# A two-block transformer on one core: load buffers on 512-byte boundaries, routing reordered, last output columns in smaller pieces

## The chip, the cores and the metric

The kernel runs as one launch on one core of a Trainium2 chip. The core has a matrix engine (PE, with its weight loads shown apart as PEld), a vector engine (DVE), a scalar engine (ACT), GpSimd (POOL) and SyncE (SP), which here only starts DMAs; 16 DMA engines carry them. Tiles live in SBUF, 128 partitions wide; matmuls write PSUM. Each engine runs its own instructions in order and waits on semaphores. The metric is the device time of one execution in microseconds (us), lower is better.

## The reference

The input is x, 256 tokens by 1024 features, float32. Two transformer blocks follow each other, and what the second one ends with matters here:

```python
x = first_block(x, ...)            # FFN, latent and stick-breaking attention, FFN, gated projection
merged = sigmoid(gate_a) * (y_attn @ w_attn_branch) + sigmoid(gate_b) * (y_ssd @ w_ssd_branch)
x = x + merged @ w_out
x = x + hier_moe(rmsnorm(x, ffn_norm), w_route_group, b_route_group, w_route_expert,
                 b_route_expert, w_gate, w_up, w_down)

def hier_moe(h, ...):              # 4 groups of 8 experts
    g_idx = argmax(h @ w_rg + b_rg)                # one group for each token
    top_v, top_i = top_k(e_logits[g_idx], 2)       # two experts of that group
    combine = group probability * softmax(top_v)
    for e in experts:                              # w_gate, w_up [1024, 256], w_down [256, 1024]
        out += (silu(h @ w_gate[e]) * (h @ w_up[e]) * combine[:, e]) @ w_down[e]
```

Each expert's three matrices are 1 MB each in float32, so the 32 experts are 96 MB, and all of it is read once.

## The kernel before

Tokens are two tiles of 128 (t = 0 and 1). Up to about 972 us the kernel computes both blocks up to `w_out_2`; its matmuls split each float32 operand in a high and a low part and run three products (`mm3`, L219 to L221). The norms of all stages use `rstd` (L137): one DVE step, a power on POOL (L142), and three small DVE steps (L144 to L147).

Then come the experts, in eight quads (q = 0 to 7) of four. SP issues their 192 loads of 512 KB (`moe_loads`, L1381; those of the last quad's `w_down` at L1378) into 32 rotating buffers: 14 from the heap, 8 halves of `raw` tiles and 10 `w4` tiles. Eight loads are in flight at a time, and when all 32 buffers hold weights the next load waits until PE has used a buffer. The order is gate and up of quad 0, then gate and up of quad q and down of quad q-1, and down of quad 7 last.

Before quad 0 can begin, the tokens must be routed. `gemm_out` (L301) computes the last projection `w_out_2`; its last four slices of the contraction (`late=4`) are done for t = 0 first and then for t = 1, so that the routing of t = 0 runs while PE still computes t = 1. `Route.feed` (L1395) takes each finished tile h (L384): a sum of squares on ACT, transposes on PE and copies to `xT` (L1406), `rstd`, the logits matmul (L1411), the logits `lg` (L1418), and the split of h in `hfh` (ACT, L1413) and `hfl` (DVE, L1421). `choose` (L1475) picks group and experts in small DVE steps: the first maximum of the group logits (`first_of`, L852), a penalty on the other groups, the two largest (`tops`, `rest`, `sel`), a running count by matmul (L1496, L1498), `mark`, a permutation matrix `perm` (L1429), and softmax weights (`ex`, `den`, `cw`, L1506 to L1516). `gather` (L1432) multiplies the split h with `perm` (L1447), 16 matmuls of 128x256 for each t, and gives each expert's tokens as `xg`. `gate_up` (L1546) begins at L1558. Where no `keep` pins it, a scheduler chooses the order of each engine's instructions when the program is built.

At the end, `down` (L1584) of quad 7 computes the 1024 output columns in two halves of 512 (L1595 to L1604). For each half it loads four pieces of 512 KB, multiplies (L1602), and `spread` (L1571) splits the result in `yh` (ACT, L1574) and `yl` (DVE, L1575), multiplies both back to token order (L1578, L1579), adds to h (L1580) and starts two output DMAs from ACT's queue (L1582).

```python
            return w.rearrange("(h p r) f -> h p (r f)", p=128, r=4)
...
            self.choose(t, lg, lambda: keep(V.tensor_tensor(hl, h, hh.bitcast(F32), op=ALU.subtract)))
            by_c = lambda z: [z[:, 512 * h:512 * h + 512].rearrange("p (q r) -> p r q", r=4)[:, r, :] for h in range(2) for r in range(4)]
```

The first line lays a gate or up matrix out for its loads; the others show that a 128x128 slice of `hfh` or `hfl` is read by `gather` with every fourth column.

## Time and profile before

| | |
|---|---|
| median of 3 runs | 1241.85 us (1241.27 to 1242.71) |
| the profiled run, its own time | 1240.49 us |
| span of the profiled execution | 1238.4 us |
| mean granted clock of PE | 0.987 |
| PE busy | 1166.7 us, 94% of the span |
| DVE, ACT, POOL busy | 765.9, 579.1, 70.9 us |
| q1, the queues of the large loads | 259.45 MB, 59.1% of 16 engines' span |

PE is busy in nearly all of the span, but the share is a mean over two parts. Up to some 972 us there are matmuls without a break; after it the loads of the experts fill the DMA engines, and PE works on what has landed. The span lacks about 2 us of the profiled run's time, which lie before and after it.

### The profile page before, as it was taken

To read this page: it belongs to the slowest core of one execution; us is meant where nothing else is said; L and a number is where in the kernel's file an instruction comes from. 1 tells how busy PE (TensorE), PEld (TensorE's weight loads), DVE (VectorE), ACT (ScalarE), POOL (GpSimd) and SP (SyncE) were. 2 spreads that over 40 slices of the span, in tenths; PEclk is the share of its full clock that TensorE was granted. 3 is DMA by queue.
4 is the path that set the end of the run, shared out by engine and by line. 5 is a ranking of instruction groups with operands and counts; after the bars stand their busy time and mean duration, and the time that the engine had idled before them with its cause. 6 is when DMAs were issued, how large, how long until landed. Compare 5 with 4: busy or idle time off the path is not lost.

```text
span 1238.4 us, 18312 instructions
## 1 busy us (share of the span) xinstructions
PE 1166.7 (94%) x7106; PEld 916.5 (74%) x7107; DVE 765.9 (62%) x1431; ACT 579.1 (47%) x946; POOL 70.9 (6%) x117
## 2 busy tenths in 40 slices
PE   6999999999999999999998899999999999797877
PEld 5888888977778788888776788898778876352422
DVE  6677747776457676764789777899786552121212
ACT  5555535456565555543654476666444321010100
POOL 2000001110000500000000200000100000000000
PEclk9999999999999999999999899999999989999999
DMA  9563754563334755475542434334754799999997
GB/s 339 185 202 116 261 172 146 177 201 121 119 119 154 206 183 187 140 250 188 193 145 102 170 129 140 107 137 146 178 187 149 284 358 397 408 409 408 408 409 268
DMA packets 105451, 266.22 MB, mean 215 GB/s; under 512 B 8597, under 2 KB 15937, under 8 KB 105361
## 3 DMA queue, kind: packets, MB, share of 16 engines
q1 hardware_dynamic: 102912, 259.45, 59.1%
q0 software_dynamic: 1728, 4.00, 1.4%
q10 hardware_dynamic: 720, 1.57, 0.3%
q8 instruction: 57, 0.93, 0.3%
q14 instruction: 34, 0.27, 0.1%
HBM read 263.95 MB, written 1.05 MB: 214 GB/s over the span
## 4 chain that ended last, share of the span: by engine, by line
PE 50%; DMA 14%; DVE 8%; issue 2%; POOL 2%; ACT 1%; DVEq 0%; POOLq 0%; SPq 0%; ACTq 0%
PE mm L219 7%; PE mm L221 7%; PE mm L220 7%; DMA wq<-in_w_up_dram 4%; DMA wq<-in_w_down_dram 3%; DMA wq<-in_w_gate_dram 2%; DVE lo L203 2%; PE mm L293 2%; PE at L293 2%; DMA raw<-in_w_gate_dram 2%; PE mm L1088 2%; DMA raw<-in_w_down_dram 2%; PE mm L1089 2%; PE mm L1090 2%; POOL r L142 1%
## 5 line engine op out<-in xcount | busy, mean ns | idle before, releaser
L203 DVE TENSOR_TENSOR lo<-raw,hi 128x1024 fp32r<-128x1024 f32 (+3 forms) x312 | 366.2, 1180 | 178.3 <-ACT hi L202 174.0
L202 ACT CAST hi<-raw 128x1024 fp32r<-128x1024 f32 (+3 forms) x312 | 316.0, 1016 | 284.3 <-PE o L220 95.3
L293 PE MATMUL mm<-x,hi 128*128 128x512 f32 x272 | 99.8, 400 | 2.9 <-DVE x L175 2.9
L219 PE MATMUL mm<-hi,xah 128*128 128x512 f32 x192 | 78.4, 409 | 2.7 <-DVE zs L1244 2.6
L142 POOL TENSOR_TENSOR r<-ms,phalf 128x1 f32<-128x1 f32 (+2 forms) x40 | 39.4, 984 | 725.7 <-DVE ms L140 720.4
L1558 PE MATMUL at<-wq,xg 128*32 128x256 f32 x736 | 63.5, 391 | 15.3 <-DMA wq<-in_w_up_dram 11.3
L294 PE MATMUL mm<-x,lo 128*128 128x256 f32 x272 | 76.3, 282 | 0.1
L221 PE MATMUL mm<-hi,xal 128*128 128x512 f32 x192 | 75.6, 394 | 0.3 <-DVE xal L175 0.3
L220 PE MATMUL mm<-lo,xah 128*128 128x512 f32 x192 | 75.6, 394 | 0.2 <-DVE ms L140 0.2
L293 PE MATMUL at<-x,hi 128*128 128x512 f32 x192 | 70.2, 392 | 0.0
L293 PEld LDWEIGHTS mm<-x,hi 128*128 128x128 f32 x272 | 51.8, 191 | 15.2 <-DVE x L175 3.5
L1558 PEld LDWEIGHTS at<-wq,xg 128*32 128x32 f32 x736 | 28.4, 112 | 43.9 <-DMA wq<-in_w_up_dram 19.4
L1088 PE MATMUL mm<-xah,hi 128*128 128x256 f32 x192 | 57.6, 300 | 3.2 <-ACT sq L957 3.2
L1568 DVE SCALAR_TENSOR_TENSOR act<-at,cg,sa 128x256 f32<-128x256 f32 x8 | 5.3, 663 | 89.3 <-ACT sa L1565 89.3
L293 PE MATMUL tp<-x,hi 128*128 128x512 f32 x160 | 59.0, 392 | 0.0
L1089 PE MATMUL mm<-xal,hi 128*128 128x256 f32 x192 | 55.9, 291 | 0.0
L1090 PE MATMUL mm<-xah,lo 128*128 128x256 f32 x192 | 55.3, 288 | 0.0
L294 PE MATMUL at<-x,lo 128*128 128x256 f32 x192 | 53.5, 278 | 0.0
L294 PEld LDWEIGHTS mm<-x,lo 128*128 128x128 f32 x272 | 51.9, 192 | 0.8 <-DVE lo L203 0.8
L1565 ACT ACTIVATE sa<-at,rs 128x256 f32<-128x256 f32 x8 | 3.8, 474 | 103.4 <-PE at L1558 74.9
L221 PE MATMUL mm<-hi,gxl 128*128 128x512 f32 x132 | 51.6, 391 | 0.0
L220 PE MATMUL mm<-lo,gxh 128*128 128x512 f32 x132 | 51.6, 391 | 0.0
(575 smaller groups left out, 2735.5 us busy)
## 6 DMA issues: line engine op xcount, KB each, us to landing
raw<-in_w_in_dram SPq DMA_DIRECT2D x50, 1024.0 KB, 4.9
raw<-in_ffn_w_in_dram SPq DMA_DIRECT2D x40, 1024.0 KB, 5.0
wq<-in_w_down_dram SPq DMA_DIRECT2D x52, 512.0 KB, 10.2
wq<-in_w_up_dram SPq DMA_DIRECT2D x48, 512.0 KB, 10.2
raw<-in_ffn_w_out_dram SPq DMA_DIRECT2D x22, 1024.0 KB, 5.1
wq<-in_w_gate_dram SPq DMA_DIRECT2D x44, 512.0 KB, 10.2
raw<-in_w_gate_dram SPq DMA_DIRECT2D x20, 512.0 KB, 10.2
raw<-in_w_out_dram SPq DMA_DIRECT2D x8, 1024.0 KB, 4.9
```

The lines of the kernel that those rows point to most:

```text
L142: G.tensor_tensor(out=r0, in0=ms, in1=phalf[:, :n], op=ALU.pow)
L202: first(S.copy(hi, part))
L203: first(V.tensor_tensor(lo, part, hi.bitcast(F32), op=ALU.subtract))
L219: PE.matmul(ps, xh, wh, start=first, stop=False)
L220: PE.matmul(ps, xh, wl, start=False, stop=False)
L221: PE.matmul(ps, xl, wh, start=False, stop=last)
L293: PE.matmul(ps[f], hi[:, c, s], sx.both[k // 2][:, :, k % 2, :], start=(k == 0), stop=False)
L294: PE.matmul(ps[f][:, 1, :], lo[:, c, s], sx.hi(k), start=False, stop=(k == KC - 1))
L1088: PE.matmul(o, hi[:, c, s], xh, start=(k == 0 and f % 2 == 0), stop=False)
L1089: PE.matmul(o, hi[:, c, s], xl, start=False, stop=False)
L1090: PE.matmul(o, lo[:, c, s], xh, start=False, stop=(k == 7 and f % 2 == 1))
L1558: PE.matmul(pg[s, n * 256:n * 256 + 256], xg[k // 4][:, k % 4, c:c + CAP], ws[j][:, r * 256:r * 256 + 256], start=(n + k == 0), stop=(n + ...
```

## The change

Seven edits, in the order of the program:

- A tile `pad` of 448 bytes in each partition, used by nothing, stands first in the constants. With the other changes of constants it moves the first address of the pools `weights` and `heap` from 96 bytes past a multiple of 512 (25184 and 98912) to a multiple of 512 (25600 and 99328), and with it all load buffers, since their sizes are multiples of 512.
- `rstd` for one column: POOL also computes `q`, minus half of the power, and DVE needs two steps after the power where it needed three.
- `w_out_2` runs with `late=5`.
- Routing: group logits and expert logits begin at columns 0 and 8 of 40; the first maximum is found by the same MAX, MEMSET and MATCH_REPLACE steps as the two best experts; nearly all of these DVE steps are pinned in program order; the softmax weights of both tiles (`weigh`) come after the routing of t = 1; the `hfl` of t = 1 comes in two halves.
- The split h is stored in chunks, so that `gather` reads each 128x128 slice contiguously; ACT's copy and DVE's subtraction now read h with a stride of 8 elements. The order of the contraction changes with it, so the gate and up loads take 4 KB out of every 8 KB, as the down loads did before.
- The last quad's down works on columns 0 to 511, 512 to 767 and 768 to 1023: four loads of 512 KB, then twice four of 256 KB, whose contiguous runs in DRAM are 2 KB and 1 KB. Six output DMAs replace four.
- POOL sets the widened `wr` and `br` and no longer writes `rev`.

```diff
+TAKEN, ABSENT = -3.0e38, 3.0e38
...
+    cp.tile([128, 112], F32, name="pad")
...
+        if n == 1:
+            q, u, r = small([128, 1], name="q"), small([128, 1], name="u"), small([128, 1], name=name)
+            G.tensor_scalar(q, r0, -0.5, None, op0=ALU.mult)
+            pin(V.scalar_tensor_tensor(u, r0, r0, ms, op0=ALU.mult, op1=ALU.mult))
+            pin(V.scalar_tensor_tensor(r, u, -3.0, q, op0=ALU.add, op1=ALU.mult))
+            return r
...
-        run(gemm_out(mx2, a["w_out_2"], 8, consume, fin))
+        run(gemm_out(mx2, a["w_out_2"], 8, consume, fin, late=5))
...
-        wr = heap([128, 8, 36], name="wr")
+        wr = heap([128, 8, 40], name="wr")
+        G.memset(wr, 0.0)
...
-        G.dma_start(g_exp.rearrange("p (h r) -> p h r", h=2), a["ffn_norm_2"].rearrange("(h p r) -> p h r", p=128, r=4))
-        br = cp.tile([128, 36], F32, name="br")
...
+        G.dma_start(g_exp, a["ffn_norm_2"].rearrange("(p c) -> p c", p=128))
...
+    LAST = [slice(0, 512), slice(512, 768), slice(768, 1024)]
...
-    def rows_of(w, what="gu"):
-
-        if what == "gu":
-            return w.rearrange("(h p r) f -> h p (r f)", p=128, r=4)
+    def rows_of(w):
+
         return w.rearrange("(p r) f -> p (r f)", p=128)
...
+            ws = []
...
                         if (q, what) == (7, "d"):
-                            src = a[nm][e // 8][e % 8].rearrange("(p r) f -> p r f", p=128)
-                            keep(nc.sync.dma_start(w.rearrange("p (r f) -> p r f", r=2), src[:, :, half * 512:half * 512 + 512]))
+                            ws.append(w)
+                            continue
                         else:
-                            src = rows_of(a[nm][e // 8][e % 8], what)
-                            keep(nc.sync.dma_start(w, src[half] if what == "gu" else src[:, half * 1024:half * 1024 + 1024]))
+                            src = rows_of(a[nm][e // 8][e % 8])
+                            keep(nc.sync.dma_start(w, src[:, half * 1024:half * 1024 + 1024]))
                         yield w
+        for i, c in enumerate(LAST):
+            n = c.stop - c.start
+            for j in range(4):
+                w = ws[4 * (i > 0) + j][:, 512 * (i > 1):][:, :2 * n].rearrange("p (r f) -> p r f", r=2)
+                e = 28 + j
+                keep(nc.sync.dma_start(w, a[NAMES[2]][e // 8][e % 8].rearrange("(p r) f -> p r f", p=128)[:, :, c]))
+                yield w
...
-            if t == 1:
+
+            chunks = lambda z: z.rearrange("p (c q) -> p c q", c=8)
+            rows = h.rearrange("p (q c) -> p c q", c=8)
+            self.hi[t], self.lo[t] = chunks(hh), chunks(hl)
+
+            def rest(c):
+                keep(V.tensor_tensor(self.lo[t][:, c], rows[:, c], self.hi[t][:, c].bitcast(F32), op=ALU.subtract))
+
+            keep(S.copy(self.hi[t], rows))
+            if t == 0:
+                rest(slice(0, 8))
+            else:
                 self.first = self.gather(0, ("mm", "mm", "mm", "o"))
                 next(self.first)
...
+            self.weigh[t] = self.choose(t, lg, lambda: [rest(slice(c, c + 4)) for c in (0, 4) if t])
+            if t == 1:
+                for weigh in self.weigh:
+                    weigh()
...
-                    pin(PE.matmul(ps[k // 2][:, k % 2, :], src[t][k], P[t],
+                    pin(PE.matmul(ps[k // 2][:, k % 2, :], src[t][:, k, :], P[t],
...
+            flat = lambda z: z.rearrange("p g e -> p (g e)")
+
+            def firsts(x, n, name):
+
+                top, rest = small([128, 8], name="tops"), small([128, x.shape[1]], name=name)
+                keep(V.max(out=top, in_=x))
+                keep(V.memset(top[:, n:], ABSENT))
+                keep(V.match_replace(out=rest, in_to_replace=top, in_values=x, imm_value=TAKEN))
+                return top, rest
+
+            gtop, grest = firsts(lg[:, :8], 1, "grest")
             pen = small([128, 4], name="pen")
-            V.tensor_scalar(pen, first_of(gl, gmax, 4, rev), -1.0, -NEG, op0=ALU.add, op1=ALU.mult)
-            flat = lambda z: z.rearrange("p g e -> p (g e)")
+            keep(V.tensor_scalar(pen, grest[:, :4], 0.5 * TAKEN, NEG, op0=ALU.is_gt, op1=ALU.mult))
...
+            top, rest = firsts(flat(ml), 2, "rest")
...
             mark = self.mark[t] = small([128, 32], name="mark")
-            V.scalar_tensor_tensor(mark, sel, -float(FAR), pr, op0=ALU.mult, op1=ALU.add)
+            keep(V.scalar_tensor_tensor(mark, sel, -float(FAR), pr, op0=ALU.mult, op1=ALU.add))
             self.perm(t, 0)
             then()
...
+            def weigh():
+
...
+            return weigh
...
-            yh, yl = heap([128, 512], FR, name="yh"), heap([128, 512], FR, name="yl")
+            n = c.stop - c.start
+            yh, yl = heap([128, n], FR, name="yh"), heap([128, n], FR, name="yl")
...
+                for piece in LAST:
+                    y = mm()[:, :piece.stop - piece.start]
                     ws = [next(loads) for _ in range(4)]
                     for i in range(5):
                         for j, c in ((i, 0), (i - 1, 1)):
                             if 0 <= j < 4:
-                                PE.matmul(y[slot(j), :], aT[:, c, slot(j)], ws[j][:, cols[c]], start=(c == 0), stop=(c == 1))
-                    spread(y, back, cols[nb], True)
+                                PE.matmul(y[slot(j), :], aT[:, c, slot(j)], ws[j][:, c, :], start=(c == 0), stop=(c == 1))
+                    spread(y, back, piece, True)
                 return
             y = [mm() for _ in range(2)]
             for c in range(2):
```

In DVE's row from the last part of h of t = 1 on (h_5538, tiles 9614 to 9632 belong to t = 1, the others to t = 0), before:

```order
L384 SCALAR_TENSOR_TENSOR h_5538<-o_9387,h_5538 128x512
L1429 TENSOR_TENSOR perm_9570<-mark_9568,marks 128x256
L1421 TENSOR_TENSOR hfl_9539<-h_5537,hfh_9538 128x1024
L1512 TENSOR_TENSOR ex_9580<-ex_9580,sel_9564 128x32
L1406 COPY xT_9616<-tp_9618 128x512
L1513 TENSOR_REDUCE den_9581<-ex_9580 128x1
L1406 COPY xT_9616<-tp_9625 128x512
L1514 TENSOR_TENSOR den_9581<-den_9581,gs_9578 128x1
L1515 RECIPROCAL den_9581<-den_9581 128x1
L1516 TENSOR_SCALAR cw_9543<-ex_9580,den_9581 128x4x8
L1407 TENSOR_TENSOR ss_9614<-ss_9614 128x1
L140 TENSOR_SCALAR ms_9632<-ss_9614 128x1
```

and now (h_5551, tiles 9620 to 9644 belong to t = 1):

```order
L393 SCALAR_TENSOR_TENSOR h_5551<-o_9412,h_5551 128x512
L1501 MEMSET tops_9575 128x6
L1413 COPY xT_9622<-tp_9624 128x512
L1502 MATCH_REPLACE rest_9576<-tops_9575,ml_9573 128x32
L1413 COPY xT_9622<-tp_9631 128x512
L1512 TENSOR_SCALAR sel_9580<-rest_9576 128x32
L1414 TENSOR_TENSOR ss_9620<-ss_9620 128x1
L143 TENSOR_SCALAR ms_9638<-ss_9620 128x1
L1519 SCALAR_TENSOR_TENSOR mark_9584<-sel_9580,at_9582 128x32
L149 SCALAR_TENSOR_TENSOR u_9643<-r_1942_9640,ms_9638 128x1
L1447 TENSOR_TENSOR perm_9586<-mark_9584,marks 128x256
L150 SCALAR_TENSOR_TENSOR r_9644<-u_9643,q_9642 128x1
```

Before, t = 0's `perm`, its `hfl` and its softmax weights stood between h and `ms` of t = 1; now only the end of t = 0's choice does, and `mark` and `perm` of t = 0 stand behind `ms`.

In PE's row from the logits of t = 1 to its gather, before (the lines left out are the other 11 matmuls of t = 0's gather; four more stood ahead of the logits):

```order
L1411 MATMUL at_9641<-wr_3819,xT_9616 128x36 x8
L1447 MATMUL mm_9653<-perm_9570,hfh_9538 128x256
...
L1528 MATMUL tp_9813<-cw_9543,perm_9570 128x9
L1538 MATMUL tp_9826<-ident,perm_9570 128x128
L1496 LDWEIGHTS before
L1496 MATMUL at_9700<-sel_9698,before 128x32
L1498 LDWEIGHTS ones
L1498 MATMUL at_9700<-sel_9564,ones 128x32
L1447 MATMUL mm_9653<-perm_9705,hfh_9650 128x256 x2
```

and now (left out: 15 more matmuls of t = 0's gather):

```order
L1514 LDWEIGHTS before
L1514 MATMUL at_9582<-sel_9580,before 128x32
L1418 MATMUL at_9648<-wr_3828,xT_9622 128x40 x8
L1465 MATMUL mm_9660<-perm_9586,hfh_9558 128x256
...
L1514 LDWEIGHTS before
L1514 MATMUL at_9702<-sel_9700,before 128x32
L1516 LDWEIGHTS ones
L1516 MATMUL at_9702<-sel_9580,ones 128x32
L1465 MATMUL mm_9660<-perm_9707,hfh_9657 128x256 x2
```

The count of t = 0 (`at_9582`) moved from ahead of the end of the projection to just ahead of t = 1's logits, and all 16 matmuls of t = 0's gather now stand between the logits and the count of t = 1. The matmuls for slot weights (L1528, L1538) left this place for one behind quad 0's gate matmuls.

In ACT's row at the end of the program, from the first piece of the last quad on, before:

```order
L1574 CAST yh_11184<-mm_11167 128x512
L1582 DMA out_dram<-h_5537 128x512
L1582 DMA out_dram<-h_5538 128x512
L1574 CAST yh_11215<-mm_11198 128x512
L1582 DMA out_dram<-h_5537 128x512
L1582 DMA out_dram<-h_5538 128x512
```

and now:

```order
L1596 CAST yh_11206<-mm_11185 128x512
L1604 DMA out_dram<-h_5550 128x512
L1604 DMA out_dram<-h_5551 128x512
L1596 CAST yh_11233<-mm_11220 128x256
L1604 DMA out_dram<-h_5550 128x256
L1604 DMA out_dram<-h_5551 128x256
L1596 CAST yh_11260<-mm_11247 128x256
L1604 DMA out_dram<-h_5550 128x256
L1604 DMA out_dram<-h_5551 128x256
```

The copy `yh` of each later piece stands behind the two output DMAs of the piece before it, now twice.

## Rows read from the trace of the kernel before

**Rows 1.** The page, part 2: GB/s moved in each of 40 slices of 30.96 us

```profile
GB/s 339 185 202 116 261 172 146 177 201 121 119 119 154 206 183 187 140 250 188 193 145 102 170 129 140 107 137 146 178 187 149 284 358 397 408 409 408 408 409 268
```

**Rows 2.** Windows: length, busy us (pieces) of PE, PEld, DVE, ACT, POOL; PEclk, DMA share, GB/s

```profile
840.00:842.00 2.00, 2.00 (x19) 2.00 (x18) 2.00 (x6) 1.05 (x1) 1.34 (x2) 1.00 0.47 174
1012.00:1014.00 2.00, 2.00 (x11) 2.00 (x10) 1.04 (x6) 0.00 (x0) 0.00 (x0) 0.50 1.04 414
1014.00:1022.00 8.00, 8.00 (x124) 4.94 (x127) 1.38 (x2) 1.68 (x4) 0.00 (x0) 0.87 0.60 213
1022.00:1030.00 8.00, 8.00 (x135) 4.62 (x131) 1.26 (x5) 2.34 (x3) 0.00 (x0) 1.00 1.00 363
```

**Rows 3.** Waits of SP's queue from 900 us on: total us, times, longest us

```profile
SPq L1381 <- PE at L1558: 13.3, 14, 9.2
```

**Rows 4.** Timeline of DVE, 1000 to 1016.5 us: start, us, engine, line, operation

```profile
1001.53 0.69 DVE L384 SCALAR_TENSOR_TENSOR h<-o,h 128x512 f32<-128x512 f32 x1
1005.72 0.15 DVE L140 TENSOR_SCALAR ms<-ss 128x1 f32<-128x1 f32 x1
1006.60 0.16 DVE L144 SCALAR_TENSOR_TENSOR u<-r 128x1 f32<-128x1 f32 x1 [0.73 <-POOL r L142]
1007.26 0.26 DVE L1418 SCALAR_TENSOR_TENSOR lg<-at,r,br 128x36 f32<-128x36 f32 x1
1009.61 0.18 DVE L1494 TENSOR_SCALAR sel<-rest 128x32 bf16<-128x32 f32 x1
1010.63 0.42 DVE L1429 TENSOR_TENSOR perm<-mark,marks 128x256 fp32r<-128x256 f32 x1
1010.98 1.22 DVE L1421 TENSOR_TENSOR hfl<-h,hfh 128x1024 fp32r<-128x1024 f32 x1
```

**Rows 5.** Timeline of PE, 1000 to 1016.5 us

```profile
1004.55 2.27 PE L1411 MATMUL at<-wr,xT 128*128 128x36 f32 x16
1010.11 0.23 PE L1496 MATMUL at<-sel,before 128*128 128x32 bf16 x1
1011.20 1.76 PE L1447 MATMUL mm<-perm,hfh 128*128 128x256 f32 x6 [0.83 <-DVE perm L1429]
1013.51 1.73 PE L1447 MATMUL mm<-perm,hfl 128*128 128x256 f32 x6
1015.66 1.04 PE L1558 MATMUL at<-wq,xg 128*32 128x256 f32 x12
```

**Rows 6.** Timeline of PE, 840 to 842 us: 128x256 matmuls with contiguous weights

```profile
840.02 0.28 PE L1089 MATMUL mm<-xal,hi 128*128 128x256 f32 x1
840.14 0.28 PE L1090 MATMUL mm<-xah,lo 128*128 128x256 f32 x1
```

**Rows 7.** Timeline of PE, 1219 to 1238.4 us

```profile
1227.25 3.16 PE L1602 MATMUL mm<-wq,aT 128*32 128x512 f32 x16
```

**Rows 8.** Timeline of ACT and its DMA queue, 1219 to 1238.4 us

```profile
1227.85 0.93 ACTq L1582 DMA_DIRECT2D out_dram<-h  x2
1230.50 0.59 ACT L1574 CAST yh<-mm 128x512 fp32r<-128x512 f32 x1 [4.70 <-DMA out_dram<-h]
```

**Rows 9.** Timeline of DVE, 1219 to 1238.4 us

```profile
1233.02 0.68 DVE L1580 TENSOR_TENSOR h<-mm,h 128x512 f32<-128x512 f32 x1
```

**Rows 10.** Windows, in the last loads (columns as in group 2)

```profile
1218.00:1220.00 2.00, 2.00 (x7) 0.52 (x4) 0.44 (x1) 0.78 (x2) 0.00 (x0) 1.00 1.05 387
```

**Rows 11.** The page, part 5: line, operation, count; busy us, mean ns; idle before

```profile
L142 POOL TENSOR_TENSOR r<-ms,phalf 128x1 f32<-128x1 f32 (+2 forms) x40 | 39.4, 984 | 725.7 <-DVE ms L140 720.4
```

**Rows 12.** Groups by line, 1000 to 1016 us: a small POOL operation

```profile
L1420 POOL COPY cw<-r 128x4 f32<-128x4 f32 x1 | 0.2, 192 | 0.6 <-DVE need L1479 0.6
```

**Rows 13.** Waits of PE over the span: total us, times, longest us

```profile
PE tp L166 <- DVE hg L365: 8.3, 2, 7.5
```

**Rows 14.** The page, part 6: DMA issues, KB each, median us to landing

```profile
wq<-in_w_down_dram SPq DMA_DIRECT2D x52, 512.0 KB, 10.2
wq<-in_w_gate_dram SPq DMA_DIRECT2D x44, 512.0 KB, 10.2
```

More of the change, by code (lines that the diff above doesn't have):

```diff
@@ L849, in ple @@
         return hn
-    def first_of(x, m, n, rev):
-        eq = small([128, n], name="eq")
-        V.scalar_tensor_tensor(eq, x, m, rev[:, :n], op0=ALU.is_equal, op1=ALU.mult)
-        top = small([128, 1], name="top")
-        V.tensor_reduce(out=top, in_=eq, axis=AX.X, op=ALU.max)
-        oh = small([128, n], name="oh")
-        V.tensor_scalar(oh, eq, top, None, op0=ALU.is_equal)
-        return oh
     def block2_consts():
@@ L1401, in feed @@
             for i, c in enumerate(halves):
-                S.activation(junk[:, c], h[:, c], AF.Square, accum_out=ss[:, i:i + 1])
+                keep(S.activation(junk[:, c], h[:, c], AF.Square, accum_out=ss[:, i:i + 1]))
                 p = tp()
@@ L1405, in feed @@
                     PE.transpose(p[:, j, :], h[:, i * 512 + j * 128:i * 512 + (j + 1) * 128], ident)
-                V.tensor_copy(xT[:, 4 * i:4 * i + 4, :], p)
-            V.tensor_tensor(ss[:, 0:1], ss[:, 0:1], ss[:, 1:2], op=ALU.add)
-            r = rstd(ss[:, 0:1], 1, D)
-            ps = at((128, 36))
+                keep(V.tensor_copy(xT[:, 4 * i:4 * i + 4, :], p))
+            keep(V.tensor_tensor(ss[:, 0:1], ss[:, 0:1], ss[:, 1:2], op=ALU.add))
+            r = rstd(ss[:, 0:1], 1, D, pin=keep)
+            ps = at((128, 40))
             for k in range(8):
@@ L1475, in choose @@
         def choose(self, t, lg, then):
[L1476 to L1482 removed]
+            before, ones = self.consts[2:4]
+            flat = lambda z: z.rearrange("p g e -> p (g e)")
[6 more added lines that the diff above has]
+            gtop, grest = firsts(lg[:, :8], 1, "grest")
             pen = small([128, 4], name="pen")
[L1484 to L1485 removed]
+            keep(V.tensor_scalar(pen, grest[:, :4], 0.5 * TAKEN, NEG, op0=ALU.is_gt, op1=ALU.mult))
             ml = heap([128, 4, 8], name="ml")
[L1487 to L1492 removed]
+            keep(V.tensor_tensor(ml, lg[:, 8:].rearrange("p (g e) -> p g e", g=4), bc(pen[:, :, None], [128, 4, 8]), op=ALU.add))
+            top, rest = firsts(flat(ml), 2, "rest")
             sel = self.sel[t] = small([128, 32], BF, name="sel")
[L1494 removed]
+            keep(V.tensor_scalar(sel, rest, 0.5 * TAKEN, None, op0=ALU.is_lt))
             pr = at((128, 32))
@@ L1595, in down @@
             if q == 7:
-                for nb in range(2):
-                    y = mm()
+                for piece in LAST:
+                    y = mm()[:, :piece.stop - piece.start]
                     ws = [next(loads) for _ in range(4)]
```

84 lines of the change are left out of this document (33 added, 51 removed).

## The prediction

> **What bounds the kernel now.** I read the GB/s row of the page first. From about 960 us to the end the DMA engines move 408 to 409 GB/s in nearly every slice [rows 1]: here the experts' loads set the time, and a matmul saved counts only if a load starts earlier for it. The one dent is slice 33. The windows show it: 213 GB/s from 1014 to 1022 us, 363 from 1022 to 1030 [rows 2]. Against 409 the first lacks 8 x (1 - 213/409) = 3.8 us of transfer, the second 0.9. The waits of SP name the cause: a load waits 9.2 us for PE at L1558 [rows 3], the first gate matmul. All 32 buffers are full, and quad 0 cannot begin before the tokens are routed. It begins at 1015.66 [rows 5]. So the start of L1558 is the point to follow; each microsecond by which it comes earlier is a microsecond of the run, until the dent is gone (3.8 us).
>
> I count from H, the end of h of t = 1, 1001.53 + 0.69 = 1002.22 [rows 4]. Before: `ms` at H + 3.5, `lg` at H + 5.04, `sel` at H + 7.4 [rows 4], count of t = 1 at H + 7.9, first matmul of t = 1's gather at H + 9.0, L1558 at H + 13.44 [rows 5].
>
> The second place is the end: the last down matmuls start at 1227.25 and take 3.16 us [rows 7], `yh` follows at 1230.50 [rows 8], the last addition ends at 1233.02 + 0.68 = 1233.70 [rows 9], then the output leaves. Up to some 972 us PE works without a break, and small edits on other engines count only where it waits.
>
> **The routing.** First DVE. Between H and `ms` the change takes out `perm` and `hfl` of t = 0 (0.42 and 1.22 us, [rows 4]) and five small steps of its softmax weights, some 0.2 us each (`lg` to `sel` is 2.35 us for 13 steps, [rows 4]); with overlap of their ends that is 2.4 us. It puts in a MEMSET, a MATCH_REPLACE and `sel` of t = 0, 0.7 us. `ms` moves from H + 3.5 to about H + 1.8, the power's answer comes 0.88 later (1005.72 to 1006.60, [rows 4]), and with `perm` of t = 0 (0.42) and one step less DVE could write `lg` at H + 3.5.
>
> Then PE, which is now late instead. The count of t = 0 stands ahead of the logits of t = 1, and it waits for `sel` of t = 0, which DVE writes behind both `xT` copies, about H + 1.7. Behind that wait stand the logits matmuls, 2.27 us [rows 5], and with them `lg`: H + 1.7 + 0.3 + 2.27 = H + 4.3, 0.75 us earlier than before and not 1.5.
>
> Next, all 16 matmuls of t = 0's gather stand between these logits and the count of t = 1. Before, 12 did, and four ran while PE had nothing else. What one costs decides, and there are two prices. Before, each stands about 0.24 us behind the one ahead of it, six in 1.73 us with the tail of the last [rows 5], at a clock of 0.50 in the window of 1012 to 1014 [rows 2]. Other 128x256 matmuls, whose weights are contiguous as these now will be, follow each other by 0.12 us at a clock of 1.00 [rows 2, 6].
> - Dear end, 0.24: gather of t = 0 to H + 8.1, count of t = 1 at H + 8.1 (0.2 later than before), first gather matmul 1.09 us behind it as before (1010.11 to 1011.20, [rows 5]), 16 matmuls of 0.24 = 3.8: L1558 at H + 13.0. Gain 0.4 us, all of it from the transposes L1538 that no longer stand inside this gather.
> - Cheap end, 0.12: gather of t = 0 to H + 6.2; now `sel` sets the count, `lg` + 2.35 = H + 6.65; `perm` ends 0.94 later (1010.11 to 1011.05, [rows 4, 5]), H + 7.6; the two halves of `hfl` (0.61 each, half of 1.22, [rows 4]) to H + 8.85; four more matmuls and the copies: L1558 at about H + 9.6. Gain 3.8 us, the whole dent.
>
> Which price holds hangs on the clock in this stretch. It was 0.50 at 1012 to 1014, and PE had waited often before that (0.83 us just ahead of 1011.20, [rows 5]); in the changed order it still waits between H and the logits. That speaks for the dear end for t = 0's part; for t = 1's part either can hold. I take the middle, **2.1 us**, and keep both ends. `late=5` gives t = 0 five slices of the projection as cover instead of four; its DVE work has all of t = 1's slices beside it, so I cost it at nothing. If its choice were late, the count of t = 0 would hold the logits by as much. The stride in ACT's copy and in `hfl`: nothing shows its price; if `hfl` took twice its 1.22, the dear end would not move, since its second half would be read at H + 11.4, about when PE gets to it.
>
> **The last columns.** The last loads carry runs of 2 KB at 387 GB/s [rows 10] where 4 KB runs moved at 409: 5% dearer. Halving the run once more should add about twice that to the last 2.1 MB: 5.4 us grow by 0.55. In return the last round on 256 columns instead of 512 is shorter: the matmuls behind the last load by about 0.85, `yh`, `yl` and the additions by 0.2, 0.3 and 0.5 (halves of their column-dependent parts). Unhindered that would be 1.3 us better. But the pieces form a chain: PE multiplies piece 2 only behind the spread of piece 1 (before, 1227.25 is just behind the first half's spread), and ACT copies `yh` of a piece only behind the output DMAs of the piece before, which wait for its additions (1227.85 + 0.93 = 1228.78, [rows 8]). Two such links instead of one: piece 2's `yh` at about 1228.8, its DMAs until about 1231.2, piece 3's `yh` then, 0.7 us **later** than today's 1230.50; from there to the last addition 2.1 instead of 3.2 us, so 1233.3 instead of 1233.7. With a shorter last DMA I take **0.6 us** gain, between 1.3 better and 0.5 worse.
>
> **`rstd`.** POOL's `q` runs beside DVE's `u`. Another small POOL step took 0.19 us [rows 12], as long as the DVE step saved; then each site gains about 0.15 us. If `q` took as long as a power (mean 0.98, [rows 11]), a site would lose 0.5. It counts where PE waits for a norm, some five places ([rows 13] holds two of them, 7.5 us at the start, most of it loading). I take **0.3 us** gain, between 0.8 better and 2.5 worse. POOL's `memset`s lie early and are covered.
>
> **The pad** only moves addresses. The nearest rows are the stream itself: 409 GB/s in steady state, 414 in its best 2 us here [rows 1, 2]. The stream of 192 loads, 100.7 MB, takes 246 us, so that difference would be 3.0 us; a loss has no reason. No row shows a transfer with another offset, and I take 0.
>
> The Trainium skill speaks for more: "DMA: Bandwidth & Descriptors", section "How a descriptor splits into AXI transactions", says that transactions start at 256-byte boundaries and that the bytes in front cost beats too. By it a 4 KB run at an offset of 96 would cost 131 beats instead of 128, an estimate of 2.3% or 5.6 us of the stream. The trace neither confirms nor denies it; the same page gives 408.7 GB/s for a lone load stream of 4 KB rows, which is this trace's rate, without saying at which offset.
>
> **The sum.** 1240.49 - 2.1 - 0.6 - 0.3 = 1237.5 against the profiled run's own time. That run lies 1.36 us under the median of 1241.85, so the forecast is 1238.9 us, 0.24% less. About 0.2% (2.5 us) is what a measurement of this kernel can tell from no change, so the forecast lies just beyond that bound.
>
> **Rivals.**
> 1. The wait moves to PE and nothing is gained at the dent: t = 0's gather at the dear price between logits and count. Then L1558 gains 0.4, the end perhaps 0.4: about 1241.0, no change. For it: the clock row and PE's order. Against: 16 contiguous weight loads. Chance 0.27.
> 2. The pad speeds up the stream: 3.0 us more by the rows' best stretch, 1235.9. For it: the stream is the bound for 246 us. Against: a rate so even that nothing in the rows points to waste. Chance 0.12. By the beats of the Trainium skill's page ("DMA: Bandwidth & Descriptors") it would be an estimated 1233.3.
> 3. The new layout slows the stream. 128 of the 192 loads now take 4 KB out of every 8 instead of one contiguous block. The last loads, which also skip, are the slower ones [rows 10]. If that were due to skipping and not to the short runs, 128 x 1.28 us (524,288 bytes at 409 GB/s) = 164 us would grow by up to 5.4%, 8.9 us: about 1247.8. It decides from 3.4% on (5.6 us), where the result turns slower by 2.5 us. Against: down loads skip in the same way already and land in 10.2 us like the gate loads [rows 14]. Chance 0.07.
> 4. The edits do what they say, but the routing is not what SP waits for: excluded by rows 3 and 5, unless another buffer is late; no chance of its own.
>
> **How the numbers follow.** Forecast 0.54, its own range 1237.0 to 1241.0, two thirds of it more than 2.5 us below 1241.85. Faster by over 0.2%: 0.54 x 0.67 + 0.12 + a little of rival 1 = 0.52. Slower: rival 3 and half of `rstd`'s bad end, 0.08. The rest, 0.40, is no change. The range of 8 in 10 takes in the forecast, rival 1 and most of rival 2: 1234.2 to 1242.6.
>
> **What would show it.** Right: L1558 starts at H + 10 to H + 13, the 8-us window behind it loses 1.5 to 3 us of transfer instead of 3.8, the steady rate stays at 408 to 409, and ACT's last `yh` begins at the end of an output DMA. Wrong: a steady rate above 411 (the pad counts) or below 405 (the layout counts), the logits of t = 1 waiting beyond H + 2.3, or `hfl` of t = 1 running past the gather's high part.

## The result and the profile after

The changed kernel takes 1236.05 us (median of 6 runs, 1232.96 to 1238.9), the kernel before in the same session 1241.56. The ratio is 0.9947, 95% interval 0.9932 to 0.9962: 5.5 us in the medians and 0.5% by the ratio faster. The forecast was 1238.9 with a range of 1234.2 to 1242.6. The profiled run took 1233.61 us, its span 1231.9 (before 1238.4). One further run of the kernel with contiguous blocks (below) took 1428.05 us at a mean granted clock of 0.751, and no figure here counts it.

The GB/s row of the page shows the first thing that the forecast did not have:

```profile
GB/s 344 185 202 122 255 173 147 176 200 125 120 113 151 195 201 178 135 253 199 176 169 71 171 138 138 137 103 141 188 184 155 220 416 418 418 417 419 418 419 252
```

Where [rows 1] had 408 to 409 there is now 416 to 419 in every slice of the steady stream (the 33rd to the 39th), and the dent of the 33rd slice is gone. The windows of the kernel after (columns as in [rows 2]) show both, and a new shallow place at the start of the stream:

```profile
974.00:980.00 6.00, 6.00 (x32) 5.03 (x31) 6.00 (x9) 3.01 (x4) 0.00 (x0) 1.00 0.91 289
1004.00:1014.00 10.00, 8.60 (x94) 7.48 (x97) 7.86 (x35) 3.04 (x11) 0.60 (x3) 1.00 1.03 414
1014.00:1022.00 8.00, 8.00 (x136) 6.32 (x132) 0.80 (x5) 2.02 (x3) 0.00 (x0) 1.00 1.03 417
1050.00:1100.00 50.00, 41.57 (x292) 18.29 (x287) 12.18 (x24) 5.46 (x11) 0.00 (x0) 1.00 1.03 418
```

The granted clock (the column before the last two) is 1.00 in the routing, 1004 to 1014. From 974 to 980 the DMA engines move 289 GB/s; before it was 406.

The routing on PE, in the timeline of the kernel after (start, duration, then the wait ahead of it):

```profile
1003.24 0.18 PE L1514 MATMUL at<-sel,before 128*128 128x32 bf16 x1 [0.94 <-DVE sel L1512]
1003.26 1.96 PE L1418 MATMUL at<-wr,xT 128*128 128x40 f32 x16
...
1007.47 0.18 PE L1514 MATMUL at<-sel,before 128*128 128x32 bf16 x1 [0.27 <-DVE sel L1512]
...
1008.50 0.95 PE L1465 MATMUL mm<-perm,hfh 128*128 128x256 f32 x6 [0.83 <-DVE perm L1447]
...
1010.51 0.50 PE L1465 MATMUL mm<-perm,hfl 128*128 128x256 f32 x2 [0.30 <-DVE hfl L1426]
...
1011.18 0.64 PE L1579 MATMUL at<-wq,xg 128*32 128x256 f32 x8
```

and the steps of DVE that it waits for:

```profile
994.85 2.07 DVE L1426 TENSOR_TENSOR hfl<-h,hfh 128x1024 fp32r<-128x1024 f32 x1
...
1000.92 0.67 DVE L393 SCALAR_TENSOR_TENSOR h<-o,h 128x512 f32<-128x512 f32 x1
...
1005.26 0.26 DVE L1435 SCALAR_TENSOR_TENSOR lg<-at,r,br 128x40 f32<-128x40 f32 x1 [0.44 <-PE at L1418]
...
1007.93 0.42 DVE L1447 TENSOR_TENSOR perm<-mark,marks 128x256 fp32r<-128x256 f32 x1
1008.27 2.19 DVE L1426 TENSOR_TENSOR hfl<-h,hfh 128x512 fp32r<-128x512 f32 x2
```

H is 1000.92 + 0.67 = 1001.59, and the first gate matmul (L1579, formerly L1558) starts at 1011.18 = H + 9.59. In [rows 4, 5] it was H + 13.44.

The end, ACT's timeline of the kernel after:

```profile
1217.57 0.59 ACT L1596 CAST yh<-mm 128x512 fp32r<-128x512 f32 x1 [4.83 <-PE mm L1624]
1220.68 0.94 ACTq L1604 DMA_DIRECT2D out_dram<-h  x2
1221.65 0.37 ACT L1596 CAST yh<-mm 128x256 fp32r<-128x256 f32 x1 [3.50 <-DVE h L1602]
1223.94 0.82 ACTq L1604 DMA_DIRECT2D out_dram<-h  x2
1224.80 0.37 ACT L1596 CAST yh<-mm 128x256 fp32r<-128x256 f32 x1 [2.78 <-PE mm L1624]
```

then PE's products of the next pieces (L1624) and the multiplications back (L1601) between them, and DVE's last addition:

```profile
1218.86 0.62 PE L1624 MATMUL mm<-wq,aT 128*32 128x256 f32 x2
1219.41 0.50 PE L1601 MATMUL o<-yl,permT 128*128 128x512 f32 x1
...
1223.49 1.08 PE L1624 MATMUL mm<-wq,aT 128*32 128x256 f32 x14
...
1226.45 0.41 DVE L1602 TENSOR_TENSOR h<-mm,h 128x256 f32<-128x256 f32 x1
```

From the first `yh` of the last quad to the end of the last addition: 1226.86 - 1217.57 = 9.29 us. Before it was 8.48 (1225.22, below, to 1233.70).

One more point lies between: the last up block, the gate and up matmuls that PE starts when the last load of an up matrix has landed. Before, with the first `yh` of the last quad, and after:

```profile
1207.62 1.91 PE L1558 MATMUL at<-wq,xg 128*32 128x256 f32 x26 [0.66 <-DMA wq<-in_w_up_dram]
1225.22 0.59 ACT L1574 CAST yh<-mm 128x512 fp32r<-128x512 f32 x1 [4.83 <-PE mm L1602]
```

```profile
1200.22 1.91 PE L1579 MATMUL at<-wq,xg 128*32 128x256 f32 x26 [0.62 <-DMA wq<-in_w_up_dram]
```

Along this chain the 6.5 us between the two spans fall into place:

| stretch | before | after | difference |
|---|---|---|---|
| start to H | 1002.22 | 1001.59 | -0.63 |
| H to the first gate matmul | 13.44 | 9.59 | -3.85 |
| first gate matmul to the last up block | 191.96 | 189.04 | -2.92 |
| last up block to the first `yh` of the last quad | 17.60 | 17.35 | -0.25 |
| first `yh` to the last addition's end | 8.48 | 9.29 | +0.81 |
| last addition to the end of the span | 4.70 | 5.04 | +0.34 |

### The profile page after: what moved, and what is told of

Read it like the earlier page. It is cut to its first block, busy times and chain, and to the rows that moved or that the text cites. A ratio compares the mean times of both kernels' runs of the same rounds, so it can differ in the third digit from the quotient of the medians.

```text
span 1231.9 us, 18388 instructions
## 1 busy us (share of the span) xinstructions
PE 1158.9 (94%) x7126; PEld 908.0 (74%) x7127; DVE 765.7 (62%) x1407; ACT 580.9 (47%) x947; POOL 82.2 (7%) x144
## 4 chain that ended last, share of the span: by engine, by line
PE 55%; DMA 11%; DVE 8%; ACT 1%; POOL 1%; issue 1%; ACTq 0%; DVEq 0%; SPq 0%; POOLq 0%
PE mm L228 8%; PE mm L230 8%; PE mm L229 8%; DMA wq<-in_w_up_dram 4%; PE mm L302 3%; DMA wq<-in_w_gate_dram 2%; DVE lo L212 2%; PE at L302 2%; PE at L1579 2%; DMA wq<-in_w_down_dram 2%; PE mm L1632 2%; PE mm L1087 2%; PE mm L1088 1%; PE tp L302 1%; PE mm L1089 1%; PE mm L303 1%
## 5 line engine op out<-in xcount | busy, mean ns | idle before, releaser
L211 ACT CAST hi<-raw 128x1024 fp32r<-128x1024 f32 (+3 forms) x312 | 315.9, 1016 | 284.9 <-PE o L229 95.0
L1579 PE MATMUL at<-wq,xg 128*32 128x256 f32 x736 | 66.9, 396 | 17.0 <-DMA wq<-in_w_up_dram 12.7
L1579 PEld LDWEIGHTS at<-wq,xg 128*32 128x32 f32 x736 | 31.2, 112 | 46.4 <-DMA wq<-in_w_up_dram 23.0
```

What stands on the lines that cost most here:

```text
L211: first(S.copy(hi, part))
L1579: PE.matmul(pg[s, n * 256:n * 256 + 256], xg[k // 4][:, k % 4, c:c + CAP], ws[j][:, r * 256:r * 256 + 256], start=(n + k == 0), stop=(n + ...
```

## Experiments

**The pad, taken back alone** (buffers at 96 bytes past a multiple of 512, as in the kernel before).

```
-    cp.tile([128, 112], F32, name="pad")
+    cp.tile([128, 8], F32, name="pad")
```

> The changed kernel with the pad cut from 448 to 32 bytes, so that the pools weights and heap begin 96 bytes past a multiple of 512, as before the change; all else is the changed kernel. Theory A, the address sets the rate of the loads: the steady rate falls from the 418 GB/s of the changed kernel's windows back to 408 to 409, and some 170 loads of 512 KB before the last gate and up load take 1.28 us instead of 1.25, so the time rises by about 5 us, to about 1241. Theory B, the rate rose for another reason (the new layout of the gate and up loads, or the routing that no longer lets the queue run dry): the steady rate stays at 418 and the time at about 1236.

Measured: 1238.31 us, ratio to before 0.9963 (0.9949 to 0.9977). The window of 1050 to 1100 reads

```profile
1050.00:1100.00 50.00, 41.19 (x280) 18.05 (x276) 11.95 (x24) 5.46 (x11) 0.00 (x0) 1.00 1.03 408
```

so the old rate is back, with the new routing unchanged (first gate matmul at H + 9.59, no dent). The address sets the rate. From the first gate matmul to the end of the span this kernel takes 225.15 us, the kernel after 220.72: 4.4 us. The interval also says that the other edits, without the pad, are worth something against the kernel before. The last up block stands here:

```profile
1203.84 3.52 PE L1579 MATMUL at<-wq,xg 128*32 128x256 f32 x26 [0.66 <-DMA wq<-in_w_up_dram]
```

**The pad alone, in the kernel before.**

```
     cp = ctx.enter_context(tc.tile_pool(name="consts", bufs=1))
+    cp.tile([128, 104], F32, name="pad")
```

> The kernel before with nothing but a pad of 416 bytes ahead of its constants, so that its load buffers begin at multiples of 512. Theory A, the address sets the rate: 418 GB/s in the steady windows instead of 409; the dent behind the routing stays at about 3.8 us since the routing is untouched; the time falls by 165 loads x 0.028 = 4.6 us, to about 1237. Theory B, another reason: 409 GB/s and no change from the kernel before (1241.6).

Measured: 1235.95 us, ratio 0.9952 (0.993 to 0.9973), two of its windows and its last up block:

```profile
1014.00:1022.00 8.00, 8.00 (x130) 4.87 (x133) 1.38 (x2) 1.68 (x4) 0.00 (x0) 0.90 0.59 205
1050.00:1100.00 50.00, 42.55 (x370) 22.60 (x362) 8.93 (x19) 3.80 (x8) 0.00 (x0) 0.93 1.03 419
```

```profile
1202.64 1.91 PE L1559 MATMUL at<-wq,xg 128*32 128x256 f32 x26 [0.61 <-DMA wq<-in_w_up_dram]
```

The dent stays (205), the rate is 419. First gate matmul (1015.33) to last up block takes 187.31 us instead of 191.96: 4.65 us by one line. That line alone gives as much in the median as the whole change. The other edits alone gave 0.9963, so the two gains do not add up. In the profiles the last up block starts at 1207.62 before, 1203.84 with all but the pad, 1202.64 with the pad alone and 1200.22 with both: on top of the pad the other edits bring 2.4 us up to there. The next experiments show where they lose it again.

**Which addresses?** The same pad at three other offsets: 224, 256 and 32 bytes past a multiple of 512.

```
-    cp.tile([128, 112], F32, name="pad")
+    cp.tile([128, 168], F32, name="pad")   (224; 48 columns for 256, 120 for 32)
```

> The changed kernel with a larger pad, so that its load buffers begin 224 bytes past a multiple of 512. Offset 0 ran at 418 GB/s in the steady windows, offset 96 at 409. Theory A, every 256-byte line that a run touches costs whole 32-byte beats from the line's start: a 4 KB run at 96 costs 131 beats and at 224 135, against 128 at 0, so 418 x 128 / 135 = 396 GB/s. Theory B, any place off a multiple of 512 costs the same: 409. The beats are those of the Trainium skill, "DMA: Bandwidth & Descriptors", section "How a descriptor splits into AXI transactions". Of the routing: the first gate matmul starts about 9.6 us after the end of h of t = 1 where the granted clock stays at 1.00, about 12.7 where it falls to 0.50.

> The changed kernel with a smaller pad, so that its load buffers begin 256 bytes past a multiple of 512. Theory A, lines of 256 bytes: 418 GB/s, as at 0. Theory B, multiples of 512 are what counts: 409 or less. Of the routing: 9.6 us from h of t = 1 to the first gate matmul at a clock of 1.00, 12.7 at 0.50.

> The changed kernel with its load buffers 32 bytes past a multiple of 512. Theory A, beats: 129 for 128, 414 to 415 GB/s. Theory B, off a line is off a line: 409. Of the routing: 9.6 us from h of t = 1 to the first gate matmul at a clock of 1.00, 12.7 at 0.50.

Measured, the window of 1050 to 1100 in that order:

```profile
1050.00:1100.00 50.00, 42.26 (x280) 18.47 (x268) 11.24 (x23) 5.46 (x11) 0.00 (x0) 0.97 1.03 408
```

```profile
1050.00:1100.00 50.00, 42.53 (x322) 18.99 (x314) 10.47 (x22) 5.46 (x11) 0.00 (x0) 0.97 1.03 418
```

```profile
1050.00:1100.00 50.00, 41.13 (x318) 18.51 (x309) 9.00 (x19) 4.95 (x11) 0.00 (x0) 1.00 1.03 408
```

Times 1238.07, 1235.38 and 1239.73 us, one run each; the rates decide here, not the times. There are two rates and nothing between: 418 at 0 and 256, 408 at 32, 96 and 224. A multiple of 256 is enough, and at these three offsets the price of missing it does not depend on by how much. Theory A, that it does, fell at both ends: it had 396 for 224 and 414 to 415 for 32.

**Two pieces instead of three at the end.**

```
-    LAST = [slice(0, 512), slice(512, 768), slice(768, 1024)]
+    LAST = [slice(0, 512), slice(512, 1024)]
```

> The changed kernel with the last quad's 1024 output columns in two halves of 512, as before the change. In the changed kernel's trace the way from the first matmul behind the last up load (1200.22) to the last addition (1226.86) is 26.6 us, in the kernel before (1207.62 to 1233.70) 26.1. Theory A, PE's chain of pieces (matmul, split, spread) is what ends last there and a third piece lengthens it: this kernel is 0.3 to 0.6 us faster than the changed one. Theory B, the smaller pieces save what the prediction said, 0.6 us: this kernel is that much slower. Either is near what three rounds can tell; the trace decides.

Measured: 1232.83 us, ratio 0.9912 (0.9881 to 0.9944). ACT, PE and DVE at the end:

```profile
1219.55 0.58 ACT L1596 CAST yh<-mm 128x512 fp32r<-128x512 f32 x1 [4.83 <-PE mm L1624]
1220.91 0.50 PE L1601 MATMUL o<-yl,permT 128*128 128x512 f32 x1
1222.17 0.94 ACTq L1604 DMA_DIRECT2D out_dram<-h  x2
1224.46 0.58 ACT L1596 CAST yh<-mm 128x512 fp32r<-128x512 f32 x1 [4.33 <-PE mm L1624]
...
1226.97 0.68 DVE L1602 TENSOR_TENSOR h<-mm,h 128x512 f32<-128x512 f32 x1
```

First `yh` to the last addition's end: 8.10 us, 1.2 less than with three pieces (9.29 in the kernel after, 9.30 in the first experiment), and more than the 0.3 to 0.6 that theory A had. The third piece costs time. This is read from the traces; the intervals of the two ratios overlap. The second surprise of this run is in the routing:

```profile
1004.00:1014.00 10.00, 9.17 (x47) 8.99 (x47) 5.69 (x27) 1.74 (x6) 1.01 (x3) 0.53 1.03 415
1014.00:1022.00 8.00, 8.00 (x134) 4.87 (x133) 2.35 (x9) 1.63 (x7) 0.00 (x0) 0.95 0.89 338
```

The same routing code got a clock of 0.50 here from about 1004.5 us on, the first gate matmul started at H + 12.72, and a dent of 338 is left. Of the eight profiles with this code four had 1.00 (H + 9.49 to 9.60) and four 0.50 (H + 12.49 to 12.72): after, offset 96, offset 224 and contiguous blocks (next) on the one side, two halves, offsets 256 and 32, and blocks with halves on the other. So this code runs at either of the two levels (2.4 and 1.2 GHz). Each of these kernels has one profile, so that one kernel changes level from run to run is not seen, but the first experiment's ten times look like it: five lie between 1236.56 and 1237.51, five between 1239.11 and 1239.99. With load buffers on a 256-byte line and the low clock, the last up block stands at 1202.10 to 1202.20 in three profiles, only some 0.5 us ahead of the pad alone.

One thing goes with the level in all eight: H was 1000.86 to 1001.64 us in the four at 1.00 and 1001.88 to 1002.10 in the four at 0.50. No experiment moved H by itself.

**Gate and up loads in contiguous blocks, as before**, with the rest of the change kept (the copies of h then read with a stride of 4 elements instead of 8).

```
     def rows_of(w, what="gu"):
+        if what == "gu":
+            return w.rearrange("(h p r) f -> h p (r f)", p=128, r=4)
...
-            rows = h.rearrange("p (q c) -> p c q", c=8)
+            rows = h.rearrange("p (h q r) -> p h r q", h=2, r=4)
```

> The changed kernel with gate and up weights again loaded as contiguous blocks of 512 KB; to fit, the chunks of the split h take every fourth column of each half, so ACT and DVE read h with a stride of 4 elements instead of 8, and the gather still reads contiguous slices. In the changed kernel the loads run at 229 to 326 GB/s from 974 to 980 us, at the start of the stream, where the kernel before moved 397 to 420; its 33rd load is issued at 1010.12 instead of 1007.52. Theory A, the layout of 4 KB out of every 8 is slow when all loads in flight take the same half: here 974 to 980 runs at 400 or more, and the time falls by some 2 us, to about 1234. Theory B, the dip has another cause (other transfers, the start itself): it stays, and so does the time. Of the stride: if each element in another 16-byte line costs, hfl of t = 0 stays at 2.07 us as with a stride of 8; if only the distance counts, it lies between 1.22 and 2.07.

Measured: 1232.01 us (1231.07 to 1235.35, 5 runs), ratio 0.992 (0.9895 to 0.9945).

```profile
974.00:980.00 6.00, 6.00 (x32) 5.03 (x31) 6.00 (x9) 2.98 (x4) 0.00 (x0) 1.00 1.00 398
...
1014.00:1022.00 8.00, 8.00 (x137) 6.54 (x132) 0.95 (x5) 2.17 (x3) 0.00 (x0) 1.00 0.99 354
```

The shallow place of 974 to 980 is gone (398 instead of 289); so loads that take 4 KB out of every 8 are slower where the stream starts, and not in the steady window (418 in both). In windows of 2 us just behind the start the lowest rate is 223 to 264 in seven kernels with such loads, 342 to 408 in six with blocks (the kernel before among them). Against the rate there that is 6 x (1 - 289/398) = 1.6 us of transfer. Why only the start is slow stays open. The stream now arrives earlier than the routing and waits for it again (354). The strided copies are as dear with a stride of 4: `hfl` 1.99, `hfh` 2.00 (2.07 and 2.03 with a stride of 8).

**Blocks and halves together.**

> The changed kernel with both edits that helped by themselves: gate and up loads as contiguous blocks, and the last columns in two halves of 512. The way from the first yh of the last quad to the last addition was 9.3 us with three pieces and 8.1 with two halves; the blocks took the dip out of the stream's start, but the first gate matmul is then waited for again. Expected: 1.2 us below the kernel with blocks alone and about 3 below the changed kernel, 1231 to 1232.5, if the two add up; if the earlier start of the stream only fills the buffers sooner and the first gate matmul decides, no better than with two halves alone, 1232 to 1233.

Measured: 1233.8 us (1229.08 to 1235.94), ratio 0.9927 (0.9906 to 0.9948), not better than either alone and above both expected ranges. The profile had the low clock in the routing (0.52 from 1004 to 1014), and the first gate matmul at H + 12.69.

With a clock of 0.50 the routing gives most of its gain back, and a spread of 7 us covers what the other edits bring.

**Filling PE's wait.** In the kernel after PE stood idle for 0.94 us ahead of L1514 although half of the operand of the score products behind it was ready. Those four products are put ahead of it; `number` and `place` are the position product and the steps behind it, split off so that the first tile's can be issued from within the second tile's.

```
                 keep(V.tensor_copy(xT[:, 4 * i:4 * i + 4, :], p))
+                if i == 0:
+                    ps = at((128, 40))
+                    for k in range(4):
+                        PE.matmul(ps, xT[:, k, :], wr[:, k, :], start=(k == 0), stop=False)
+                    if t == 1:
+                        self.number()
```

> The kernel after, with one thing moved: the first half of the second tile's score products (L1418, four of the eight products) is put ahead of the position product of the first tile (L1514) in PE's order. In the profile of after PE stood idle for 0.94 us just ahead of L1514, with that half's operand ready (xT copied by 1002.34) and the product of a small matrix stopping it. Theory (the clock falls to 0.50 in some runs because PE stands idle there): the gap ahead of L1514 is filled, the granted clock is 1.00 through the stretch, scores are ready 0.4 us sooner, first gate product at H + 9.2 (H is the end of h of the second tile; 9.6 in after), the times bunch at the low end of after's (1232.0 to 1233.5, where after spread over 1233.0 to 1238.9). Rival (the fall is settled earlier or elsewhere): the clock is 0.50 in some runs as before, first gate product at H + 12 in those, and the times spread over 5 to 6 us as after's did, around 1235.5.

Measured: 1234.08 us (1231.91 to 1235.44), ratio 0.9935 (0.9922 to 0.9948). PE's timeline, H = 999.73 + 0.67 = 1000.40:

```profile
1001.21 1.09 PE L1418 MATMUL at<-wr,xT 128*128 128x40 f32 x8
...
1002.35 0.19 PE L1521 MATMUL at<-sel,before 128*128 128x32 bf16 x1
...
1009.66 0.64 PE L1592 MATMUL at<-wq,xg 128*32 128x256 f32 x8
```

The wait is gone and the first gate matmul starts at H + 9.26, 0.33 sooner, with the clock at 1.00. The times did not bunch as the theory wanted: three of the six lie between 1234.98 and 1235.44, above its 1233.5.

The next kernel has these moved products, the contiguous blocks and the two halves together.

> The three changes that helped alone, together: gate and up loads in contiguous blocks, last 512 columns' pieces as two halves of 512, and the first half of the second tile's score products ahead of L1514. Theory: clock 1.00, first gate product at H + 9.2, stream at 418 GB/s from its start, first yh of the last quad to the last addition 8.1 instead of 9.3 us: after's low end 1233.0 less 1.2 (pieces), 0.3 (scores) and up to 1 (start of the stream) = 1230.5 to 1231.5, spread under 3 us. Rival (the clock falls as before whatever PE's order): 1229 to 1236, as the same kernel without the moved products spread.

Measured: 1229.4 us (1229.14 to 1232.56, 5 runs), ratio 0.9903 (0.9888 to 0.9919): the fastest of all, its interval clear of the kernel after's (0.9932 to 0.9962). It is faster than the theory had, with a spread of 3.4 us instead of under 3, and it also lies inside the rival's range. The clock is 1.00, the first gate matmul starts at H + 9.14, the stream is at 415 from 974 on, and it waits a little for the routing (356 from 1014 to 1022). Against the same kernel without the moved products four of five runs now lie within 1.1 us, and the median is 4.4 us lower, far more than 0.33. That speaks for the idle time having something to do with the clock. It doesn't show it: each kernel has one profile, the kernel after had that idle time and kept 1.00, the times of the experiment above did not bunch, and H lay at 1000.40 and 1000.61 in these two profiles, on the side of H that had gone with 1.00 before.

**The weights of the gather with a stride again**, in the new order of steps (hi and lo stored as in the kernel before, loads in contiguous blocks to fit).

```
-            keep(S.copy(self.hi[t], rows))
+            keep(S.copy(hh, h))
...
-                    pin(PE.matmul(ps[k // 2][:, k % 2, :], src[t][:, k, :], P[t],
+                    pin(PE.matmul(ps[k // 2][:, k % 2, :], src[t][k], P[t],
```

> The kernel after with the high and low parts of h stored in h's own order as in before, so that the gather's products load their weights with a stride of four elements (the gate and up loads are the contiguous blocks of before, to fit that order). Everything else of the new routing order stays. Theory (the routing gain is the contiguous weights at least as much as the order): the gather's products of the first tile take 0.22 to 0.24 us apart also at clock 1.00 (0.12 in after), those of the second tile the same, hfl and hfh take 1.2 and 1.0 us again (2.07 and 2.03 in after), first gate product at H + 11.5 to 12.5 whatever the clock, times 1234.5 to 1236.5. Rival (the order alone brings it): H + 9.6 to 10, times as with the contiguous blocks alone, 1231 to 1235.

Measured: 1235.0 us (1233.41 to 1237.91), ratio 0.9937 (0.9921 to 0.9952). First the kernel after's weight loads for the gather, then this kernel's (ns, least, median, most):

```profile
L1465 PEld LDWEIGHTS mm<-perm,hfh x60: 186/192/192, 1005.0 to 1147.4; 128*128 128x128 f32 x60
```

```profile
L1466 PEld LDWEIGHTS mm<-perm,hfh x60: 308/332/337, 1007.2 to 1155.1; 128*128 128x128 f32 x60
...
1010.43 0.37 PE L1466 MATMUL o<-perm,hfl 128*128 128x256 f32 x1
1010.64 0.40 PE L1466 MATMUL o<-perm,hfh 128*128 128x256 f32 x1
1010.88 0.40 PE L1466 MATMUL o<-perm,hfl 128*128 128x256 f32 x1
...
1016.20 1.08 PE L1580 MATMUL at<-wq,xg 128*32 128x256 f32 x8
```

H is 1003.65 here, the first gate matmul at H + 12.55: the theory held within 0.05 us, the rival (H + 9.6 to 10) fell. The stride makes a weight load 0.33 us long where a contiguous one takes 0.19 at a clock of 1.00, and the matmuls follow each other by 0.21 to 0.24 us just after the clock came back to 1.00 (0.12 in the kernel after). The copies cost 1.03 again. So the order alone does not bring H + 9.6.

The kernel with two halves has the other combination, contiguous weights at a clock of 0.50:

```profile
1006.97 0.41 PE L1465 MATMUL mm<-perm,hfh 128*128 128x256 f32 x1
1007.18 0.41 PE L1465 MATMUL mm<-perm,hfl 128*128 128x256 f32 x1
```

There they follow each other by 0.21 us, and the weight loads take 0.33 us too. So the gather is fast only with contiguous weights and the upper clock together. The kernel before shows the same: its next gather, from 1033 to 1041 us at a clock of 1.00, went at 0.23 us for each matmul. How much of this run's 3 us the clock alone took isn't shown, since it stood at 0.50 for part of this stretch.

## Why the prediction came out as it did

The time fell inside the range and on the forecast's side, 2.85 us below the forecast, and rival 2's 1235.9 is nearest to it. Of the sum behind it one term held at its two ends, two failed and one could not be tested.

- **What bounds.** Right. The stream of loads and the first gate matmul set the time, and the longest wait of SP for it shrank from 9.2 [rows 3] to 2.4 us. "Each microsecond by which it comes earlier is a microsecond of the run" was too much: against the pad alone the first gate matmul comes 4.15 us earlier (1015.33 to 1011.18) and the last up block 2.42. What is missing, 1.7 us, is about what the shallow start takes; that it is the same was not shown.
- **Routing** (2.1 us, ends 0.4 and 3.8): both ends are real, 3.85 in the profile of after at a clock of 1.00 and 0.7 to 1.0 at 0.50 (H + 12.49 to 12.72 against the 13.0 that was worked out). No profile lies near the middle that was taken; the eight fall near the two ends, four each, and the dear one is rival 1's routing. The 0.24 of the dear end was put down to the clock, but the kernel before's strided weights took 0.23 at a clock of 1.00 as well. Contiguous ones take 0.12 at 1.00 and 0.21 at 0.50, so the clock does decide for the new kernel, with a dear end 0.3 to 0.5 us better than worked out. The cheap end came out to 0.01 us by luck, two errors that cancel: `perm` of t = 1 ended at H + 6.76 instead of 7.6, because the logits started at H + 1.7 and not 2.0, took 1.96 us and not 2.27, and `lg` to `sel` 1.98 and not 2.35; and `hfl`'s halves took 2.19 us together instead of 1.22. They ended at H + 8.87 (forecast 8.85).
- **The stride** in ACT's copy and in `hfl` had no row, and "twice its 1.22" was only weighed for the dear end. It is 1.7 times for `hfl`, 2.07 instead of 1.22, and just under twice for `hfh`, 2.03 instead of 1.03. At the cheap end PE waits 0.30 us for it, which the forecast named as a sign against it.
- **Last columns** (0.6 us gain): failed in sign. 0.81 us worse than before, 1.2 worse than two halves at the same load rate. The step that failed is "piece 3's `yh`, 0.7 us later", which puts the third `yh` 5.98 us behind the first. It comes 7.23 behind; from there to the end it takes 2.06, as forecast (2.1). With two halves the last `yh` comes after 4.91: 2.32 later, of which the smaller piece then gives back only 1.1. The link was the one that the forecast named: the third `yh` starts at 1224.80, where ACT has issued the two output DMAs of the piece before (1223.94 + 0.82 = 1224.76), and its products end just before that, at 1223.49 + 1.08 = 1224.57. What was too small is the length of a link, 3.6 and 2.4 us in the forecast, 4.08 and 3.15 in the trace. In the new order PE has two products of the next piece ahead of L1601, which starts 1.84 us behind `yh` (1219.41 - 1217.57) instead of 1.36 with two halves (1220.91 - 1219.55), and the output DMAs wait for what follows it. A piece of half the width costs 3.15 us in that chain, not half of 4.91.
- **The pad** (0): failed, and in the medians it is the larger part of the result. The rate went from 409 [rows 1] to 418, worth 4.65 us between the first gate matmul and the last up block by the pad alone. The step that failed is the choice of the value: the stream ran evenly at 409, which was taken as a sign of nothing wasted, but a tax on every transfer is even too. The rival had the mechanism, with 3.0 us from the best 2 us of the rows, too small, and a chance of 0.12; the sign that the forecast gave for it, a steady rate above 411, came. The beats of the Trainium skill ("DMA: Bandwidth & Descriptors", "How a descriptor splits into AXI transactions") gave an estimated 5.6 us for the stream at this offset: near the 4.65 that was measured. The runs agree with its boundary of 256 bytes and disagree with its price by offset.
- **The layout of gate and up** (rival 3, 5.4% of the stream): the steady rate did not suffer (418). It costs at the start of the stream alone, 1.6 us of transfer, a case that neither the forecast nor the rival had.
- **`rstd` and `late=5`** (0.3 us): H came 0.63 us earlier, but it lay between 1000.86 and 1002.10 in the eight profiles with the same routing code. The term is neither shown nor refuted, and was not tried alone.

So it is partly luck that the range held: the pad's missing 4.65 us paid for a lost gain at the end, the shallow start and the runs with a low clock. In the median the pad alone matches the whole gain (0.9952 and 0.9947); the other edits without it come to 0.9963, and with it their gain is mostly lost again.

## What to carry to other kernels

Where loads bound a stretch, look at the byte address of their buffers first: a pool that starts off a 256-byte line can tax a perfectly even stream, and the profile shows that only as a plateau that could be higher. Before splitting the last piece of work more finely, follow the chain through every in-order engine: a smaller piece shortens only what scales with its width. Where a term has two prices that hang on the clock, forecast the two, not their middle, and look for the same work at the other level before a price is put down to the clock.

## What the runs showed of the hardware

- Loads of 4 KB rows into buffers at 0 or 256 bytes past a multiple of 512 run at 418 to 419 GB/s, at 32, 96 or 224 at 408 to 409: 2.4% less, whichever of the three it is.
- Reading fp32 with a stride of 4 or 8 elements about doubles an ACT copy (1.03 to between 2.00 and 2.24 us for 128x1024), and DVE's subtraction goes from 1.22 to 1.99 or 2.07; both strides cost about the same. A weight load of 128x128 with a stride of 4 takes PE 0.33 us instead of 0.19 at a clock of 1.00, and its matmuls of 128x256 then stand 0.21 to 0.24 us apart instead of 0.12. At 0.50 the contiguous load takes 0.33 us too, and they stand 0.21 apart.
- Loads that take 4 KB out of every 8 KB of DRAM ran at 223 to 264 GB/s in their slowest 2 us at the start of the stream (seven kernels), contiguous blocks at 342 to 408 (six); in the steady stream both ran at 418.
- The same routing code got TensorE's upper level in four profiles and the lower in four, for the same 10 us. PE had been idle for 0.94 us just ahead of the place in all eight, and H was the later one in the four at the lower level (1001.88 us or later against 1001.64 or earlier). What decides between them stays open.
